# Twelve tiles of the second input layer as seven products, the convolution on VectorE, and the mixing between attention's layers

## The chip, the cores and the metric

One NeuronCore of one Trainium2 chip runs the whole program. The metric is the time of one execution on the device, in microseconds. The kernel before took 2616.39, 2611.67 and 2616.32 us in three runs; their median is 2616.32 us. All times below that come from a trace are of one profiled execution, which took 2621.87 us itself.

## The reference

Two transformer-like blocks stand behind each other, on 1024 tokens of 1024 features, in float32. The first has a state-space branch with a gated linear unit (GLU), an attention that lets each query look at the 256 best keys only (top-k of an index score), and a gated feed-forward layer (FFN). The second, which most of the change is about, has one wide input layer whose columns feed three branches:

```python
def second_block(x, ...):
    h = rmsnorm(x, norm_g)
    p = h @ w_in                                  # 1024 x 7688
    gate_pre, a_in, a_z, b_uv, b_z, q, k, v, c_z, f_pre = split_columns(p)
    gates = sigmoid(gate_pre + b_gate)            # 3 x 1024 columns
    # a: convolution of 31 taps over the tokens, a layer norm, a gate
    a = a_in[..., :512] * sigmoid(a_in[..., 512:])
    a = causal_depthwise_conv(a, conv_w, conv_b)
    y_a = (silu(layernorm(a)) * silu(a_z)) @ w_a
    # b: gMLP; tokens are mixed within chunks of 128
    u, v_b = split(b_uv)
    mixed = einsum("gts,bnsgc->bntgc", tril(w_s), chunks(rmsnorm(v_b))) + b_s
    y_b = (u * mixed * silu(b_z)) @ w_b
    # c: attention of 8 heads of 64 with a decay from the forget gate f_pre
    y_c = (fox_attention(rmsnorm(q), rmsnorm(k), v, cumsum(log_sigmoid(f_pre + b_f)))
           * silu(c_z)) @ w_c
    merged = g_a * y_a + g_b * y_b + g_c * y_c
    return x + merged @ w_out
```

## The kernel before, in words

**Arithmetic.** A float32 operand is split into a high and a low part of a shorter type (`split`: ScalarE copies the high part, VectorE or GpSimd subtracts it for the low part), and a product is three matmuls, high by high, high by low, low by high (`mm3`, L159 is its matmul, L167 is a transpose on TensorE). The helpers `act` (ScalarE, L130 to L132), `tt`, `stt` and `ts` (VectorE, L122, L125 and L119, or GpSimd where it is given as the engine) and `load` (a DMA on SP's queue, for stores too) record nearly every other operation.

**Layers.** A tile is 128 output features by 1024 tokens. `linear` makes one tile in 8 k-blocks x 2 halves of 512 tokens x 3 passes = 48 matmuls, into an accumulator `pl`, of which there are two. `wino` makes two tiles at once with 7 instead of 8 block products (a scheme of Strassen's kind), 7 x 4 x 3 = 84 matmuls into accumulators `pw`; each such job needs sums of weight blocks, split in high and low (`wino_weights`: tiles `vh`, `vl`, `s12`, `s34`), and its results are put together from accumulators and copies of them (`snap`). `linear_t` makes an output with tokens on the partitions, in groups of 256 columns of 192 matmuls. Four accumulators of 512 columns (`p`, from `p1()`) are shared by `linear_t`, by transposes and by the convolution's sums.

**What sets the order.** The program is written as one thread with side threads: a generator `self.aside` is advanced by `next` at fixed places, once per tile in `linear`, twice per job in `wino`, twice per group in `linear_t`. `together` mixes side threads at a given number of steps per call. A scheduler then orders the instructions of each engine by its own simulated times. Extra edges (`later`) keep a load or an operation behind a matmul, `self.pace` or `self.mark`.

**The first block's GLU** (`glu`, 16 tiles of 24 matmuls) runs with the side thread `attention1`: it loads and forms the heads' operands, then `topk`, then `attend`. The side thread is advanced by twelve steps during the GLU; what is left of it runs after. In `attend`, each step is a unit (head, block of 128 queries): `logits` (two or more matmuls into `pl`, softmax), `turn` (transposes of the weights), `weigh` (their product with the values).

**The second block** runs in this order: `conv_in` (the inputs of the convolution); `plain_gates` (8 tiles by `linear`: az, which is a_z, and c_z, which goes to the memory `fd`); `gates2` (24 tiles of gates by 12 seven-product jobs, with the convolution of tiles 0 and 1 as side thread); `fox` (attention's k, q and v by `linear_t`; the norms of k and q are generators in a list `pending`, which each group's eviction advances by `advance`); `gmlp` (branch b's v by `linear_t`, then z and u, 8 tiles by `linear`, with the mixing on TensorE between them); `branch` b. From `fox` to branch b the side thread is the convolution of tiles 2 and 3 (`conformer`), the gate of branch a (`conformer_gate`) and `keep_x2`, which transposes the block's input back to tokens. Then branch a, attention, branch c and the output layer follow.

**The convolution** (`conv`) runs one tap per instruction: 31 taps by two halves of 512 tokens are 62 operations on VectorE per tile, into an accumulator `p`. With `both` set (tiles 2 and 3), half the taps go to ScalarE (a scaled copy into `ct`) and GpSimd (an addition into `cy`).

Of the kernel before, what the change touches and what calls it, by code (L numbers as in the profile page):

```python
# [40 lines left out]
def blocks(x, c=128):  # L41
    return x.rearrange("p (b c) -> p b c", c=c)
# [26 lines left out]
class Core:  # L69
# [1532 lines left out]
    def keep_x2(self):  # L1602
# [17 lines left out]
    def fox(self, hh, hl):  # L1620
# [74 lines left out]
        for j, (c0, gain) in enumerate(((6656, self.v["k_norm_g_2"]), (6144, gq))):  # L1695
            for g in range(2):
# [30 lines left out]
                start(unit_norm(g, j, gain, x, ss))  # L1727
        for g in range(2):
# [11 lines left out]
            self.linear_t(self.wraw(w, 0, 8, 7168 + 256 * g, 256), 8, hh, hl, ev_v)  # L1740

    def plain_gates(self, hh, hl, norm):
# [4 lines left out]
        def ev(dst, scale):  # L1747
            def f(m, p):
                z = self.pg("gst", bufs=2)
                self.mark = self.act(z, p, AF.Tanh, scale=0.5)  # L1750
                self.stt(z, z, 1.0, p, OP.add, OP.mult)
                if scale != 1.0:
                    self.act(z, z, scale=scale)
                self.load(dst(m), z)
# [11 lines left out]
    def gates2(self, x4, first):  # L1766

# [3 lines left out]
        for pair in range(12):  # L1771
# [11 lines left out]
            jobs.append((lambda pair=pair: self.wino_weights(w, 256 * pair), ev))  # L1783
        self.wino(jobs, x4, first)
# [113 lines left out]
    def gmlp(self, hh, hl):  # L1898
# [5 lines left out]
        for g in range(2):  # L1904
            def ev_v(i, p):
                x = v[i][:, :, 256 * g:256 * g + 256]
# [6 lines left out]
        def mix(t):  # L1913
            if t == 0:
                self.tt(ss[:, 0], ss[:, 0], ss[:, 1], OP.add)
                r = self.rsqrt_cols(ss[:, 0], 512)
                for i in range(8):
                    x = v[i // 2][:, i % 2]
                    self.act(x, x, scale=r[:, i:i + 1])
            yield  # L1920
            mx = self.pg("bb", bufs=4)
            for s in range(2):
                q = blocks(self.p1())
                for i in range(4):
# [281 lines left out]
```

## Time and profile before

| | |
|---|---|
| runs | 2616.39, 2611.67, 2616.32 us, median 2616.32 |
| the profiled execution, its own time | 2621.87 us |
| its span in the trace | 2620.2 us |
| granted TensorE clock, mean | 0.984 |
| instructions | 35143 |
| seven products of the second block | 1720.2 to 1954.5 us |
| k, q and v of attention | 1954.5 to 2095.9 us |
| branch b's v | 2095.9 to 2155.4 us |
| z, u and the mixing | 2155.4 to 2266.4 us |
| branch b | 2266.4 to 2315 us |

PE is TensorE's matmul row, PEld its weight loads, DVE is VectorE, ACT ScalarE, POOL GpSimd, SP the queue that issues the DMAs. A group of instructions reads as line, engine, operation, output<-inputs by the program's names, shape, count, busy time, mean duration of one, and then the idle time of the engine just before it with what ended that. A matmul's duration in the trace overlaps that of the next, so the time of many is read from the stretch that they fill. In a table of waits, "PE pl L159 <- DVE small L1182: 8.8, 1, 8.8" says that TensorE's matmul of line 159 into the tile pl waited 8.8 us in one piece for VectorE's operation of line 1182 on the tile small. PEclk is the clock granted to TensorE as a share of full speed.

### The profile page before, as it was taken

Reading aid. Unit: us, or ns where it says so; the run is one execution under the profiler, and the core shown is the slowest. Engines: PE = TensorE matmul, PEld = TensorE weight load, DVE = VectorE, ACT = ScalarE, POOL = GpSimd, SP = SyncE. Lnnn points to the kernel's source line nnn. Section 1 sums busy time; section 2 is a strip of 40 time slices with the busy share of each in tenths; the row PEclk is TensorE's granted clock in tenths of the full one; section 3 lists DMA queues with packets and bytes.
Section 4 is the critical chain, followed back from the end, with each engine's and each line's share of the span. In section 5 each row is a group of like instructions: output and inputs, shape, how many; then the busy total and the mean of one; then the engine's idle time right before and its main releaser. Section 6 shows DMA issues by size and latency. Waiting matters only on the chain. (4 is left out here: it accounts for less than half of the span.)

```text
span 2620.2 us, 35143 instructions
## 1 busy us (share of the span) xinstructions
PE 2515.9 (96%) x12849; PEld 2119.9 (81%) x12849; DVE 1653.9 (63%) x2882; ACT 1129.7 (43%) x2144; POOL 847.9 (32%) x889
## 2 busy tenths in 40 slices
PE   6998999979999999999999999999999999999999
PEld 4877887768878788888888878888889997887887
DVE  6844889868894844444553367248768737548861
ACT  5323686828834433333322244234345433108830
POOL 2698441456500024444200120022318710005500
PEclk9999999989999999999999999999999999999999
DMA  7544453555294322222632244233362522586442
GB/s 256 158 152 139 143 167 112 192 168 132 73 332 154 124 90 89 70 91 81 223 135 85 87 131 149 85 105 121 113 206 77 166 77 73 183 235 156 135 159 83
DMA packets 272188, 360.37 MB, mean 138 GB/s; under 512 B 43948, under 2 KB 210552, under 8 KB 272016
## 3 DMA queue, kind: packets, MB, share of 16 engines
q1 hardware_dynamic: 270640, 356.89, 42.5%
q0 software_dynamic: 1152, 1.21, 0.3%
q8 instruction: 101, 1.65, 0.3%
q14 instruction: 71, 0.58, 0.1%
q10 hardware_dynamic: 224, 0.03, 0.0%
HBM read 262.65 MB, written 93.32 MB: 136 GB/s over the span
## 5 line engine op out<-in xcount | busy, mean ns | idle before, releaser
L130 ACT CAST wh<-wr 128x512 fp32r<-128x512 f32 (+1 forms) x308 | 170.7, 594 | 325.1 <-PE pl L159 125.9
L159 PE MATMUL pl<-uh,wh 128*128 128x512 f32 x672 | 266.6, 397 | 1.1 <-ACT uh L132 1.1
L159 PE MATMUL pl<-uh,wl 128*128 128x512 f32 x672 | 264.6, 394 | 0.6 <-DVE wl L122 0.6
L159 PE MATMUL pl<-ul,wh 128*128 128x512 f32 x672 | 263.9, 393 | 0.0
L122 POOL TENSOR_TENSOR s<-wq 128x512 f32<-128x512 f32 x60 | 84.8, 1415 | 480.1 <-DMA wq<-in_w_in_dram 268.6
L122 DVE TENSOR_TENSOR wl<-wr,wh 128x512 fp32r<-128x512 f32 (+1 forms) x260 | 179.1, 719 | 66.4 <-ACT wh L130 55.2
L122 DVE TENSOR_TENSOR snap<-pw,snap 128x512 f32<-128x512 f32 x90 | 61.9, 690 | 206.2 <-PE pw L159 116.9
L159 PE MATMUL pw<-xtl,vh 128*128 128x512 f32 x480 | 186.7, 389 | 0.0
L159 PE MATMUL pw<-xth,vl 128*128 128x512 f32 x480 | 185.3, 389 | 0.0
L159 PE MATMUL pw<-xth,vh 128*128 128x512 f32 x480 | 185.3, 389 | 0.0
L119 POOL TENSOR_SCALAR L<-L,small 128x128 f32<-128x128 f32 (+7 forms) x128 | 95.2, 747 | 259.8 <-DVE small L1186 253.1
L122 POOL TENSOR_TENSOR sqa<-sqa,sqn 128x512 f32<-128x512 f32 (+1 forms) x19 | 31.8, 1686 | 388.5 <-ACT sqn L132 206.8
L159 PEld LDWEIGHTS pl<-uh,wl 128*128 128x128 f32 x672 | 127.8, 190 | 27.7 <-DVE wl L122 1.1
L159 PE MATMUL p<-wth,uh 128*128 128x256 f32 x512 | 146.6, 287 | 3.1 <-DVE xsl L125 3.1
L159 PEld LDWEIGHTS pl<-uh,wh 128*128 128x128 f32 x672 | 127.6, 190 | 26.9 <-ACT uh L132 1.2
L159 PEld LDWEIGHTS pl<-ul,wh 128*128 128x128 f32 x672 | 127.9, 190 | 26.2 <-DVE ul L125 0.5
L159 PE MATMUL p<-wtl,uh 128*128 128x256 f32 x512 | 145.4, 284 | 0.0
L159 PE MATMUL p<-wth,ul 128*128 128x256 f32 x512 | 145.4, 284 | 0.0
L130 ACT COPY snap<-pw 128x512 f32<-128x512 f32 x90 | 52.6, 587 | 207.5 <-PE pw L159 196.6
L159 PE MATMUL pw<-uh,vh 128*128 128x512 f32 x360 | 140.0, 389 | 0.0
L159 PE MATMUL pw<-ul,vh 128*128 128x512 f32 x360 | 140.0, 389 | 0.0
L159 PE MATMUL pw<-uh,vl 128*128 128x512 f32 x360 | 136.6, 389 | 0.0
(448 smaller groups left out, 7264.0 us busy)
## 6 DMA issues: line engine op xcount, KB each, us to landing
wr<-in_w_in_dram SPq DMA_DIRECT2D x64, 512.0 KB, 4.8
wmod<-in_w_mod_dram SPq DMA_DIRECT2D x48, 512.0 KB, 6.3
wr<-in_w_out_dram SPq DMA_DIRECT2D x24, 512.0 KB, 6.2
wq<-in_w_in_dram SPq DMA_DIRECT2D x24, 512.0 KB, 5.2
gtd<-gst SPq DMA_DIRECT2D x24, 512.0 KB, 3.1
g_th<-gtd SPq DMA_DIRECT2D x24, 512.0 KB, 5.8
fd<-f_th SPq DMA_DIRECT2D x22, 512.0 KB, 3.4
f_th<-fd SPq DMA_DIRECT2D x22, 512.0 KB, 5.1
```

The costliest lines, as they stand in the source:

```text
L119: return (eng or self.nc.vector).tensor_scalar(out=out, in0=a, scalar1=s1, scalar2=s2, op0=op0, **kw)
L122: return (eng or self.nc.vector).tensor_tensor(out=out, in0=a, in1=b, op=op)
L130: return self.nc.scalar.copy(out, a)
L159: self.tick = self.nc.tensor.matmul(out, a, b, start=start, stop=stop, skip_group_check=True)
```

## The change

Five edits stand in it:

- Twelve tiles that `linear` made are now made by `gates2` in six more seven-product jobs (18 instead of 12): b_z (two jobs), u (two jobs) and c_z (two jobs). The product silu(b_z) * u is stored in a new memory `bf` and loaded back for the mixing; `plain_gates` keeps the four tiles of az.
- The convolution runs on VectorE alone, all 62 taps per tile. Three of its four tiles run beside the seven products (at 0.7 steps per call, was two tiles at 0.75), the last one in `conformer`.
- `gmlp` only makes branch b's v and returns the mixing as a generator, which `fox` puts into `pending`; it runs before attention's v, and the mixing between that layer's groups.
- `attention1` yields once more, between `topk` and `attend`.
- `keep_x2` loads one step ahead.

```diff
@@ keep_x2
-        for k in range(8):
+        ahead = []
+        def fetch(k):
             x = self.pg("h", bufs=8)
             self.load(x, self.hd2[k], self.pace)
             self.ts(x, x, fg[:, k:k + 1])
+            ahead.append(x)
+        fetch(0)
+        yield
+        for k in range(8):
+            x = ahead.pop(0)
+            if k < 7:
+                fetch(k + 1)
@@ fox
                 start(unit_norm(g, j, gain, x, ss))
+        start(self.gmlp(hh, hl, advance))
...
+        while pending:
+            advance()
@@ plain_gates
-        self.linear(w, [(4096 + 128 * t, 128) for t in range(4)], 8, hh, hl, ev(lambda m: self.az[m], 1.0))
-        self.linear(w, [(7680 + 128 * t, 128) for t in range(2)], 8, hh, hl, ev(lambda m: self.fd[m, 3, 0], 0.5))
+        self.linear(w, [(4096 + 128 * t, 128) for t in range(2)], 8, hh, hl, ev(0))
         first = self.wino_weights(w, 0, ref=self.tick)
-        self.linear(w, [(7680 + 128 * t, 128) for t in range(2, 4)], 8, hh, hl, ev(lambda m: self.fd[m + 2, 3, 0], 0.5))
+        self.linear(w, [(4096 + 128 * t, 128) for t in range(2, 4)], 8, hh, hl, ev(2))
@@ gates2
+        self.bf = self.dram([4, 128, T], "bf")
+        def silu(t, p, more):
+            if more is None:
+                more = p
+            else:
+                self.tt(more, p, more, OP.add)
+            self.mark = self.act(t, more, AF.Tanh, scale=0.5)
+            self.stt(t, t, 1.0, more, OP.add, OP.mult)
+        for pair in range(2):
...
+            def ev_z(m, s, p, more, g=g):
+                if g[m] is None:
+                    g[m] = self.pg("gst", bufs=2)
+                silu(g[m][:, 512 * s:512 * s + 512], p, more)
+            def ev_u(m, s, p, more, g=g, pair=pair):
+                t = g[m][:, 512 * s:512 * s + 512]
+                if more is None:
+                    self.tt(t, t, p, OP.mult)
+                else:
+                    self.tt(more, p, more, OP.add)
+                    self.tt(t, t, more, OP.mult, self.nc.gpsimd)
+                if (m, s) in ((0, 1), (1, 0)):
+                    self.load(self.bf[2 * pair + m], g[m])
+            jobs.append((lambda pair=pair: self.wino_weights(w, 5632 + 256 * pair), ev_z))
+            jobs.append((lambda pair=pair: self.wino_weights(w, 4608 + 256 * pair), ev_u))
+        for pair in range(2):
...
+            def ev_c(m, s, p, more, g=g, pair=pair):
...
+                silu(t, p, more)
+                self.act(t, t, scale=0.5)
+                if (m, s) in ((0, 1), (1, 0)):
+                    self.load(self.fd[2 * pair + m, 3, 0], g[m])
+            jobs.append((lambda pair=pair: self.wino_weights(w, 7680 + 256 * pair), ev_c))
@@ gmlp
-        def mix(t):
...
-        for t in range(4):
-            self.linear(w, [(5632 + 128 * t, 128)], 8, hh, hl, ev_z)
-            self.linear(w, [(4608 + 128 * t, 128)], 8, hh, hl, ev_u)
+        def mix():
+            self.tt(ss[:, 0], ss[:, 0], ss[:, 1], OP.add)
+            r = self.rsqrt_cols(ss[:, 0], 512)
...
+            for _ in range(4):
+                yield
+            for t in range(4):
+                f = self.pg("gz", bufs=2)
+                self.load(f, self.bf[t], self.pace)
+                mx = self.pg("bb", bufs=4)
+                for s in range(2):
...
+                self.tt(mx, mx, f, OP.mult)
+                self.bb.append(mx)
+                yield
+        return mix()
@@ conv
-        taps = range(30, -1, -2 if both else -1)
-        odd = list(range(29, -1, -2)) if both else []
...
-            for n, k in enumerate(taps):
+            for n, k in enumerate(range(30, -1, -1)):
...
-                        else:
-                            z = self.pg("ct", bufs=2)
-                            i = self.act(z[:, s:], at[:, :T - s], scale=wk)
-                            self.tt(y2[:, s:], y2[:, s:], z[:, s:], OP.add, gp)
...
-                if n % (4 if both else 8) == (3 if both else 7) and n < len(taps) - 1:
+                if n % 8 == 7:
                     yield
@@ conformer
-        yield from self.conv(2, True)
         x = self.cx
-        for t in range(2):
-            x[t] = self.pg("cx", bufs=4)
-            self.load(x[t], self.cyd[t], self.pace)
-        yield from self.conv(3, True)
...
+        for n, _ in enumerate(self.conv(3, True)):
+            if n == 3:
+                for t in range(3):
+                    x[t] = self.pg("cx", bufs=4)
+                    self.load(x[t], self.cyd[t], self.pace)
...
@@ run
             self.topk(self.sc)
+            yield
             yield from self.attend(self.heads1)
...
-        self.aside = self.together(((None for t in range(2) for _ in self.conv(t, False)), 0.75))
+        self.aside = self.together(((None for t in range(3) for _ in self.conv(t, False)), 0.7))
...
         self.fox(hh, hl)
-        self.gmlp(hh, hl)
```

**How the order moves, first place: TensorE, at the end of the GLU.** yl and yh are the GLU's inputs, wh and wl its weights, akh, akl and aqq the keys and queries of the first attention. Before, the first logits stand 96 matmuls ahead of the GLU's end:

```order
L159 MATMUL pl<-yl,wh 128x512
L159 MATMUL pl<-yh,wl 128x512
L159 MATMUL pl<-akh,aqq 128x256
L159 MATMUL pl<-akl,aqq 128x256
L159 MATMUL pl<-yh,wh 128x512
L159 MATMUL pl<-yl,wh 128x512
L159 MATMUL pl<-yh,wl 128x512
```

Now:

```order
L159 MATMUL pl<-yh,wh 128x512
L159 MATMUL pl<-yl,wh 128x512
L159 MATMUL pl<-yh,wl 128x512
L159 MATMUL pl<-akh,aqq 128x256
L159 MATMUL pl<-akl,aqq 128x256
L159 MATMUL pl<-akh,aqq 128x256
L159 MATMUL pl<-akl,aqq 128x256
L159 MATMUL pl<-akh,aqq 128x384
```

The first two logits matmuls have moved behind the last of the GLU, where those of the next unit follow them at once.

**Second place: GpSimd's queue (POOL), during attention's keys and queries.** wtl is the low part of a weight group, xraw the raw keys and queries, which the norm's factor is multiplied into there. Before:

```order
L122 TENSOR_TENSOR cy<-cy,ct 128x1017
L122 TENSOR_TENSOR cy<-cy,ct 128x1015
L122 TENSOR_TENSOR wtl<-wr,wth 128x1024
L122 TENSOR_TENSOR cy<-cy,ct 128x1013
L122 TENSOR_TENSOR cy<-cy,ct 128x1011
L122 TENSOR_TENSOR xraw<-xraw,small_16105 128x1024 x2
L122 TENSOR_TENSOR cy<-cy,ct 128x1009
L122 TENSOR_TENSOR cy<-cy,ct 128x1007
```

Now:

```order
L122 TENSOR_TENSOR xraw<-xraw,small_16711 128x1024 x2
L122 TENSOR_TENSOR wtl<-wr,wth 128x1024
L122 TENSOR_TENSOR xraw<-xraw,small_16711 128x1024 x2
L122 TENSOR_TENSOR sqa<-cx 128x1024
L122 TENSOR_TENSOR sqa<-sqa,cx 128x1024
L122 TENSOR_TENSOR wtl<-wr,wth 128x1024
L122 TENSOR_TENSOR xraw<-xraw,small_16711 128x1024 x2
```

The additions of the convolution are gone; weight splits, the norms' products and the two sums of the layer norm are left.

**Third place: VectorE, the chain of small operations behind the first group of keys** (the forget gate's and the first norm's; ca and p are the convolution's input and sum). Before:

```order
L119 TENSOR_SCALAR small_5047<-small_5047 128x64
L1637 RECIPROCAL small_5047<-small_5047 128x64
L1723 TENSOR_REDUCE small_5047<-sqk 128x8
L122 TENSOR_TENSOR small_5047<-small_5047 128x64
L119 TENSOR_SCALAR small_16105<-small_5047 128x32
L122 TENSOR_TENSOR small_5047<-small_5047 128x64
L119 TENSOR_SCALAR small_16105<-small_16105 128x32
```

Now:

```order
L125 SCALAR_TENSOR_TENSOR p_16585<-ca,small_5039,p_16585 128x502
L119 TENSOR_SCALAR small_5039<-small_5039 128x64
L119 TENSOR_SCALAR small_16711<-small_5039 128x32
L125 SCALAR_TENSOR_TENSOR p_16585<-ca,small_5039,p_16585 128x501
L1646 RECIPROCAL small_5039<-small_5039 128x64
L119 TENSOR_SCALAR small_16711<-small_16711 128x32
L125 SCALAR_TENSOR_TENSOR p_16585<-ca,small_5039,p_16585 128x500
L122 TENSOR_TENSOR small_5039<-small_5039 128x64
L119 TENSOR_SCALAR small_16711<-small_16711 128x32
L125 SCALAR_TENSOR_TENSOR p_16585<-ca,small_5039,p_16585 128x499
```

A tap of the convolution now stands between nearly every two operations of the chain.

## Rows read from the trace of the kernel before

**Rows 1.** The page: busy time, share of the span, and instructions of each engine.
```profile
PE 2515.9 (96%) x12849; PEld 2119.9 (81%) x12849; DVE 1653.9 (63%) x2882; ACT 1129.7 (43%) x2144; POOL 847.9 (32%) x889
```

**Rows 2.** TensorE's groups, 1633 to 1954 us: busy, mean ns | idle before.
```profile
L159 PE MATMUL pw<-xtl,vh 128*128 128x512 f32 x192 | 74.7, 389 | 0.0
...
L159 PE MATMUL pl<-uh,wh 128*128 128x512 f32 x128 | 49.8, 389 | 0.0
```

**Rows 3.** Windows by stage: us, busy of each engine (count), PEclk, DMA share, GB/s.
```profile
core 0: us, PE busy (x) PEld busy (x) DVE busy (x) ACT busy (x) POOL busy (x), PEclk, DMA share, GB/s
1633.13:1720.17 87.04, 87.04 (x385) 72.10 (x384) 25.68 (x27) 19.17 (x25) 8.51 (x6) 1.00 0.29 97
1720.17:1940.40 220.23, 220.23 (x973) 182.44 (x972) 163.00 (x215) 92.45 (x141) 60.48 (x44) 1.00 0.35 113
1954.50:2095.90 141.40, 131.60 (x1084) 130.80 (x1083) 105.91 (x165) 74.34 (x98) 103.00 (x45) 0.98 0.42 137
2095.90:2155.40 59.50, 59.50 (x500) 59.50 (x499) 20.34 (x26) 18.34 (x48) 6.49 (x3) 1.00 0.26 76
2155.40:2266.40 111.00, 105.87 (x515) 88.97 (x513) 70.54 (x94) 34.33 (x48) 4.77 (x2) 0.97 0.31 95
```

**Rows 4.** TensorE's waits in the GLU, 465 to 583 us: us, times, longest.
```profile
PE pl L159 <- DVE small L1182: 8.8, 1, 8.8
PE pl L159 <- POOL aqq L122: 3.3, 1, 3.3
```

**Rows 5.** TensorE's waits, 1954.5 to 2315 us.
```profile
PE p L167 <- POOL xraw L122: 5.3, 1, 5.3
PE pl L167 <- ACT diag L130: 4.1, 1, 4.1
PE p L159 <- DVE xsl L125: 3.1, 1, 3.1
PE pl L167 <- DVE small L125: 1.4, 1, 1.4
```

**Rows 6.** Windows behind two waits, and of the first attention.
```profile
558.40:563.80 5.40, 5.40 (x13) 4.25 (x14) 1.10 (x2) 0.42 (x2) 4.22 (x5) 0.51 0.74 272
582.90:715.60 132.70, 119.60 (x811) 104.56 (x809) 111.88 (x318) 113.45 (x269) 84.03 (x140) 0.97 0.45 114
2075.10:2079.30 4.20, 4.16 (x20) 4.16 (x21) 2.10 (x5) 3.01 (x4) 4.15 (x2) 0.51 0.63 182
```

**Rows 7.** VectorE's groups beside the seven products, and the FFN's activation (f_th).
```profile
L125 DVE SCALAR_TENSOR_TENSOR p<-ca,small,p 128x512 f32<-128x512 f32 x60 | 45.1, 752 | 1.2
L122 DVE TENSOR_TENSOR vl<-s,vh 128x1024 fp32r<-128x1024 f32 x22 | 32.2, 1462 | 3.2 <-ACT vh L130 3.0
L122 DVE TENSOR_TENSOR snap<-pw,snap 128x512 f32<-128x512 f32 x35 | 24.1, 690 | 46.2 <-PE pw L159 27.0 <-ACT snap L130 18.9
L122 DVE TENSOR_TENSOR vl<-wq,vh 128x512 fp32r<-128x512 f32 x33 | 21.8, 685 | 1.3 <-ACT vh L130 1.3
...
L125 DVE SCALAR_TENSOR_TENSOR f_th<-f_th,snap x27: 677/695/1782, 960.7 to 1283.7; 128x512 f32<-128x512 f32 x27
```

**Rows 8.** A window of one job's length, VectorE alone.
```profile
1758.20:1777.30 19.10, 17.38 (x25) 1.00 0.37 111
```

**Rows 9.** TensorE's timeline, the matmul behind the first logits.
```profile
558.34 0.80 PE L159 MATMUL pl<-yh,wh 128*128 128x512 f32 x1 [8.77 <-DVE small L1182]
```

**Rows 10.** Tiles cy and wtl: count, ns least/median/most, first and last start.
```profile
L122 POOL TENSOR_TENSOR cy<-cy,ct x28: 2337/2393/4356, 1965.2 to 2097.4; 128x1021 f32<-128x1021 f32 x2, 128x1019 f32<-128x1019 f32 x2, 128x1017 f32<-128x1017 f32 x2, 128x1015 f32<-128x1015 f32 x2
...
L122 DVE TENSOR_TENSOR wtl<-wr,wth x7: 1220/2048/3461, 1944.3 to 2109.7; 128x1024 fp32r<-128x1024 f32 x7
```

**Rows 11.** VectorE's timeline: start, us; how a norm's chain opens, at two places.
```profile
2034.14 0.60 DVE L119 TENSOR_SCALAR small<-small 128x32 f32<-128x32 f32 x3
...
2063.46 5.04 DVE L119 TENSOR_SCALAR small<-small 128x32 f32<-128x32 f32 x3
```

**Rows 12.** VectorE's groups, 1954 to 2100 us: the forget gate's running sum.
```profile
L1652 DVE TENSOR_TENSOR_SCAN kin<-kiw,small 8x1024 f32<-8x1024 f32 x1 | 3.3, 3295 | 0.0
```

More of the change, by code (lines that the diff above doesn't have):

```diff
@@ L1905, in ev_v @@
             def ev_v(i, p):
+                advance()
                 x = v[i][:, :, 256 * g:256 * g + 256]
@@ L1911, in gmlp @@
         self.bb = []
-        def mix(t):
[L1914 to L1924, printed above, removed]
-                    self.mm(q[:, i], v[2 * s + i // 2][:, i % 2, t * 128:(t + 1) * 128], wst[:, t * 128:(t + 1) * 128])
-                self.stt(blocks(mx[:, 512 * s:512 * s + 512]), q, self.v["gmlp_norm_g_2"][:, t:t + 1],
-                         wst[:, None, 512 + 128 * t:640 + 128 * t].to_broadcast([128, 4, 128]), OP.mult, OP.add)
-            self.bb.append(mx)
-            yield
@@ L1930, in gmlp @@
-        steps = (None for t in range(4) for _ in mix(t))
-        self.hold = []
-        def ev_z(m, p):
-            th = self.pg("gz", bufs=2)
-            self.act(th, p, AF.Tanh, scale=0.5)
-            self.stt(th, th, 1.0, p, OP.add, OP.mult)
-            self.hold.append(th)
-            next(steps)
-        def ev_u(m, p):
-            th = self.hold.pop(0)
-            self.tt(th, th, p, OP.mult)
-            next(steps)
-            t = len(self.bb) - 1
-            self.tt(self.bb[t], self.bb[t], th, OP.mult)
-            self.show(f"bb{t}", self.bb[t])
@@ L1947, in gmlp @@
-        for t in range(4):
-            self.linear(w, [(5632 + 128 * t, 128)], 8, hh, hl, ev_z)
-            self.linear(w, [(4608 + 128 * t, 128)], 8, hh, hl, ev_u)
+        def mix():
+            self.tt(ss[:, 0], ss[:, 0], ss[:, 1], OP.add)
+            r = self.rsqrt_cols(ss[:, 0], 512)
+            for i in range(8):
+                x = v[i // 2][:, i % 2]
+                self.act(x, x, scale=r[:, i:i + 1])
+            for _ in range(4):
[5 more added lines that the diff above has]
+                for s in range(2):
+                    q = blocks(self.p1())
+                    for i in range(4):
+                        self.mm(q[:, i], v[2 * s + i // 2][:, i % 2, t * 128:(t + 1) * 128], wst[:, t * 128:(t + 1) * 128])
+                    self.stt(blocks(mx[:, 512 * s:512 * s + 512]), q, self.v["gmlp_norm_g_2"][:, t:t + 1],
+                             wst[:, None, 512 + 128 * t:640 + 128 * t].to_broadcast([128, 4, 128]), OP.mult, OP.add)
+                self.tt(mx, mx, f, OP.mult)
+                self.bb.append(mx)
+                self.show(f"bb{t}", mx)
+                yield
@@ L1978, in conv_in, with conv @@
             part(2, s)
-    def conv(self, t, both):
-        gp, cw = self.nc.gpsimd, self.cw
+    def conv(self, t, keep):
+        cw = self.cw
         at = self.pg("ca", bufs=4)
@@ L1986, in conv @@
         y = self.pg("cx", bufs=4)
-        taps = range(30, -1, -2 if both else -1)
-        odd = list(range(29, -1, -2)) if both else []
-        if both:
-            y2 = self.pg("cy", bufs=2)
-            self.later(gp.memset(y2[:, 0:1], 0.0), self.pace)
         for h in range(2):
@@ L2002, in conv @@
                 self.later(i, self.pace)
[L2003 to L2020 removed]
+                if n % 8 == 7:
+                    yield
+            self.act(y[:, c0:c0 + 512], acc)
             if h == 1:
                 self.show(f"conv{t}", y)
[L2023 removed]
+                if keep:
                     self.cx[t] = y
@@ L2031, in conformer @@
         gp = self.nc.gpsimd
[L2032 removed]
         x = self.cx
[L2034 to L2041 removed]
+        for n, _ in enumerate(self.conv(3, True)):
[3 more added lines that the diff above has]
+                    self.load(x[t], self.cyd[t], self.pace)
+                total = self.pg("sqa", bufs=4)
+                for y in (x[0], total):
+                    self.later(self.tt(total, y, x[1] if y is x[0] else x[2], OP.add, gp), self.pace)
+            yield
         self.tt(total, total, x[3], OP.add)
@@ L2126, in attention1 @@
             self.topk(self.sc)
+            yield
             yield from self.attend(self.heads1)
```

34 lines of the change are left out of this document (10 added, 24 removed).

## The prediction

> **What bounds the kernel now.** I read the page first: TensorE is busy for 96% of the span and VectorE for 63% [rows 1]. A busy matmul row is not yet a full engine, since rows overlap, so I take the price of a matmul from its pitch. The groups of the stretch that the change touches have no idle time before them, neither in the plain tiles (pl) nor in the tiles by seven products (pw) [rows 2]. In the windows by stage, 384 plain matmuls fill 87.04 us and 972 of the seven products 220.23 us [rows 3]: 0.2267 us each, in both. There, only fewer matmuls save time. Elsewhere TensorE stands still, and I looked for where: its own waits name 8.8 and 3.3 us in the GLU of the first block [rows 4] and 5.3, 4.1, 3.1 and 1.4 us between the end of the seven products and branch b [rows 5]. After a wait the granted clock is low for a while: 5.40 us at 0.51 hold 13 matmuls [rows 6], which at the pitch above take 2.9. So a wait costs its length and some half-speed matmuls (1.2 instead of 2.4 GHz).
>
> **The change, part by part.**
>
> *Seven products for twelve tiles.* A plain tile is 48 matmuls (8 k, 2 halves, 3 passes), so 576 go; six jobs of 84 come, 504. 72 x 0.2267 = **16.3 us less**, if the new jobs run without idle time as the old ones do.
>
> What has to hide beside them is VectorE's work. A job with a gate's activation has, from the rows of VectorE [rows 7]: two wide splits (1.46) and three narrow ones (0.685), 5.0 us; two additions of a snap (0.69), 1.4; four products of the activation (0.695, the row f_th of the FFN), 2.8; and its share of the convolution. Three parts of 62 taps over 36 calls at 0.7 steps of 8 taps are about 11 taps a job, at 0.752, 8.4 us. Together 17.6 us in the 19.04 us that 84 matmuls take: 92%. One old stretch of that length already carries 17.38 us [rows 8], and TensorE never waited there. So I cost it at nothing; the cover that is left is 1.4 us a job. The other queues have room: POOL is busy 60 of 220 us and ACT 92 [rows 3], and get four products of 512 columns (1.4 us each, 60.48 / 44) and some 24 activations (0.7 us, 92.45 / 141). SP's queue gets four stores and four loads of 512 KB, at DMA shares of 0.26 to 0.42 there.
>
> The Trainium skill, in "Perfetto Trace Analysis", section "Optimizing Scalar/DVE Operations", advises the opposite of the convolution's move: where VectorE is saturated, hand work to ScalarE or GpSimd. By it the six full jobs would lose time; the rival on VectorE below works out how much.
>
> *The added yield.* The twelfth step of the first attention now ends with top-k; the first logits, two matmuls, stand behind the GLU's last 142 matmuls instead of ahead of its last 96, as the first pair of pieces of the order shows. Today those two wait 3.3 us for POOL's aqq, and the next matmul 8.8 us, because the logits hold one of two accumulators until VectorE is through with top-k; it starts at 558.34 [rows 4, 9]. The 13 matmuls that follow at half clock cost 5.40 - 13 x 0.2267 = 2.5 us [rows 6]. All three go: 14.6 us. VectorE is through with top-k by 558, and the GLU, which now ends where attention's stretch begins at 582.9, would end at about 568.3, so nothing is late there. What comes back is the first unit of attention, which is not yet done when the others start. It costs at least nothing and at most a mean unit, 132.7 / 63 = 2.1 us (8 heads by 8 blocks, less this one) [rows 6]; it is the smallest of its head, so I take half, 1.1. **13.5 us less**, 12.5 to 14.6.
>
> *The convolution leaves POOL and ACT.* In the stretch of keys and queries, 28 additions of about 2.4 us on POOL go [rows 10], and as many scalings on ACT. VectorE's taps there stay: 62 for one tile instead of 2 x 32 for two. The rows show what the additions did. The three small operations that open VectorE's chain for a norm take 0.60 us at 2034 and 5.04 us at 2063 [rows 11]; POOL has no addition at the first place and a run of them at the second. A split of 1.22 us took up to 3.46 beside them [rows 10]. That chain is what the wait of 5.3 us hung on. The waits in this stretch sum to 13.9 us [rows 5], and the half clock behind them costs 2.1 us (half of 4.20 at 0.51) [rows 6] and 3.3 us (3% of 111) in the stage of z and u [rows 3]: 19.3 us in all. How much goes?
>
> The 5.3 with its clock should go. The 4.1 is a transpose placed too close behind a chain of small operations; in the new order 57 matmuls of 256 columns stand between, 6.8 us at 59.50 / 500 = 0.119 a piece [rows 3], and VectorE's chain is 12 operations of about 0.2 and three others, 5 us with ACT's copy; it should go, barely. The 1.4 goes, since its transposes now stand 63 matmuls later. The 3.1 is a matmul without an accumulator, since two convolution sums and two transposes hold all four. That stays, and between the two pieces it waits for VectorE now has four taps, a split, a reduction and a scan (3.3 [rows 12]), some 9 us; I put it at 5, and 2 for the clock behind. So 12 of 19 go. Bounds: nothing goes (0), or all (19). **12 us less.**
>
> A risk stands in the third pair of pieces: the taps are now mixed into the first norm's chain, ten of them at 0.75 us in 13 us. POOL's product follows, at most an addition's 2.4 [rows 10], so its transposes are ready some 15 to 17 us after the first group ends, where TensorE reaches them after 144 matmuls, 17.1 us.
>
> *The mixing* keeps its 64 matmuls and moves between the groups of attention's v. Its inputs pass through VectorE (two sums of 0.75, a product and a split of 1.22, and v's own split of 0.69, by the rows of like width [rows 7, 10]: 4.6 us) in the 5.7 us of 48 matmuls of 256 columns: no wait, no gain. *The loads of keep_x2* start one earlier, but its eight steps come closer together, at the start of branch b: three passes of VectorE each, about 0.7 a 512 columns, beside the two of a branch tile, 4.5 us in the 5.4 of its 24 matmuls. Nothing, up to 5 us of loss.
>
> Sum: 16.3 + 13.5 + 12 = 41.8 us. The profiled execution took 2621.87 us, so 2580.1; it lies 5.55 us above the median of the runs (2616.32), which gives **2574.5 us** as the median after.
>
> **The rivals.**
> 1. *The stretch of keys and queries gives nothing*: taps in the norm chains, and the closer steps of keep_x2, cost what POOL's additions did. For it: VectorE is busy 106 of 141 us there already [rows 3]. Against: the waits are tied to operations beside the additions. 2616.3 - 16.3 - 13.5 = 2586.5.
> 2. *VectorE becomes the bound of the six full jobs.* If both wide splits met POOL at 3.46 instead of 1.46, a job needs 21.6 us against 19.04: 2.6 x 6 = 15 us back, 2590. It decides from 1.4 us more than I count. Against: 17.38 us passed without a wait [rows 8]. This is what the skill's advice would come to.
> 3. *Slower: the same in all 18 jobs.* The taps fall in all of them; if the splits late by that much stop TensorE in each, 2.6 x 18 = 47 us come back: 2621.5. It needs VectorE over 19.04 us in every job, and today the mean is 163.00 / 220.23 of it, 14.1 [rows 3].
> 4. *The yield moves the wait, and the attention ends no sooner*, because it is bound from its start by VectorE and ScalarE (112 and 113 of 132.7 us [rows 6]). Against: TensorE is busy 120 of the same 132.7, and VectorE is idle when the GLU ends. 2588.
>
> **How the numbers follow.** Forecast 0.60 (its own range 2566 to 2584: 19 or 3 of the 19.3 us go, and the yield's bounds), rival 1 0.20, rival 2 0.10, rival 4 0.06, rival 3 0.04. The range of 8 in 10 takes in the forecast and the first two rivals and reaches past both: down by the 4 us or so that the three runs differ among themselves (2566 - 4), up by the same and most of keep_x2's 5 (2590 + 8): 2562 to 2598. A measurement of this kernel can tell about 0.2%, 5 us, from no change. All but rival 3 and the far end of rival 2 are faster by more: 0.93 faster, 0.03 same, 0.04 slower.
>
> **What would show it.** Seven products: 1476 pw matmuls in one block of about 335 us at 0.2267, no waits of pw. Yield: no wait of TensorE in the GLU, its end near 568 us, first block's attention still about 133 us. Stretch: no operation of a norm's chain above 0.3 us, one wait for xsl of 3 to 6 us. I am wrong if pw matmuls wait for vl or snap, or if the waits between the seven products and the third branch sum to more than 15 us.

## The result, and the profile after

The changed kernel takes 2577.81 us (median of four runs, 2574.54 to 2580.82), the kernel before 2616.36 in the same comparison: 0.986 of the time, 95% interval 0.9848 to 0.9872, or 38.6 us less. The forecast was 2574.5, with a range of 2562 to 2598. The profiled execution took 2580.82 us (before: 2621.87), so the two traces differ by 41.1 us of span, against a sum of 41.8.

The total hides that two of its three terms were far off, in opposite directions. The page of the changed kernel, for [rows 1]:

```profile
PE 2495.0 (97%) x12777; PEld 2106.2 (82%) x12777; DVE 1697.6 (66%) x2968; ACT 1120.5 (43%) x2152; POOL 821.5 (32%) x889
```

72 matmuls are gone. VectorE carries 43.7 us more work, GpSimd 26.4 less. To see where the time went I cut both traces at the same places of the program and compare stretches. The kernel before, the GLU, and all from the last of the seven products to the end of branch b (the first attention stands in [rows 6]):

```profile
core 0: us, PE busy (x) PEld busy (x) DVE busy (x) ACT busy (x) POOL busy (x), PEclk, DMA share, GB/s
465.24:582.89 117.65, 103.00 (x438) 83.17 (x437) 86.44 (x138) 60.95 (x133) 65.26 (x34) 0.94 0.53 173
1940.49:2314.98 374.49, 358.69 (x2402) 331.18 (x2401) 224.25 (x320) 139.65 (x214) 116.93 (x52) 0.98 0.43 139
```

The changed kernel: the GLU, the first attention, the plain tiles, the seven products, and the stretch behind them to the end of branch b:

```profile
466.86:580.72 113.86, 102.22 (x436) 82.70 (x434) 86.65 (x134) 60.28 (x129) 64.13 (x31) 0.96 0.54 178
580.72:713.18 132.46, 119.56 (x814) 105.14 (x813) 111.69 (x322) 114.83 (x272) 84.97 (x143) 0.97 0.43 115
1628.25:1671.77 43.52, 43.52 (x194) 36.04 (x192) 15.97 (x15) 7.90 (x10) 9.29 (x7) 1.00 0.29 97
1671.77:2006.33 334.56, 334.56 (x1478) 277.03 (x1476) 255.70 (x331) 135.35 (x209) 106.75 (x74) 1.00 0.33 109
2006.33:2272.71 266.38, 264.59 (x2018) 254.47 (x2016) 184.49 (x302) 97.29 (x169) 43.94 (x21) 1.00 0.57 187
```

From the stretch before I take off the 384 plain matmuls of z and u, 87.05 us at 0.2267, since they now stand as seven products:

| step | forecast | by the two traces |
|---|---|---|
| twelve tiles as seven products | 16.3 | 16.3 (43.52 + 334.56 against 87.04 + 220.32 + 87.05) |
| GLU and first attention (the yield) | 13.5 | 4.0 (113.86 + 132.46 against 117.65 + 132.70 [rows 6]) |
| end of the seven products to the end of branch b | 12 | 21.1 (266.38 against 374.49 - 87.05) |
| everything else | 0 | -0.3 |

The last row hides a spread: the way from the first attention into the FFN, which no edit touches, is 2.5 us shorter in the second trace (235.55 against 238.02), and other parts are longer. So a difference of 2 us in one stretch of two traces shows nothing by itself.

*Seven products.* 1476 matmuls fill 334.56 us, 0.2267 each as before, and no row of pw has a wait. VectorE's heaviest new jobs (windows of one job's length, as [rows 8]):

```profile
1918.50:1937.50 19.00, 18.14 (x22) 1.00 0.20 56
1937.50:1956.50 19.00, 16.93 (x24) 1.00 0.32 110
```

The job that I had put at 17.6 us takes 17 to 18, and TensorE does not notice.

*The GLU.* Of its waits, for [rows 4], one has taken the place of the two:

```profile
PE pl L159 <- POOL wl L122: 10.6, 3, 8.6
```

*Keys, queries, v, mixing, branch b*, for [rows 5]: of the waits there nothing over 1.5 us is left, and that one is new and small. The clock column says 1.00, where it was 0.98.

```profile
PE pl L159 <- DVE wtl L122: 1.5, 1, 1.5
```

### The profile page after: what moved, and what is told of

It is laid out like the page before. It is cut to its first block, busy times and chain, and to the rows that moved or that the text cites. A ratio compares the mean times of both kernels' runs of the same rounds, so it can differ in the third digit from the quotient of the medians.

```text
span 2579.1 us, 35104 instructions
## 1 busy us (share of the span) xinstructions
PE 2495.0 (97%) x12777; PEld 2106.2 (82%) x12777; DVE 1697.6 (66%) x2968; ACT 1120.5 (43%) x2152; POOL 821.5 (32%) x889
## 3 DMA queue, kind: packets, MB, share of 16 engines
q0 software_dynamic: 1152, 1.21, 0.3%
## 4 chain that ended last, share of the span: by engine, by line
PE 78%; DVE 10%; POOL 4%; ACT 3%; DMA 2%; issue 2%; SPq 0%; POOLq 0%; DVEq 0%; ACTq 0%
PE pw L159 26%; PE pl L159 24%; PE p L159 24%; PE p L167 3%; DVE tk_j L119 2%; POOL s_F L122 1%; POOL s_ct L122 1%; POOL s_E L122 1%; ACT L L132 1%; DVE s_d L122 1%; DVE h L125 1%; DMA yd<-s_X 0%; PE pl L167 0%; DMA aq<-qd 0%; DVE wl L122 0%
## 5 line engine op out<-in xcount | busy, mean ns | idle before, releaser
L159 PE MATMUL pw<-xtl,vh 128*128 128x512 f32 x576 | 224.1, 389 | 0.0
L159 PE MATMUL pw<-xth,vh 128*128 128x512 f32 x576 | 222.8, 389 | 0.0
L159 PE MATMUL pw<-xth,vl 128*128 128x512 f32 x576 | 222.3, 389 | 0.0
L122 DVE TENSOR_TENSOR wl<-wr,wh 128x512 fp32r<-128x512 f32 x236 | 160.0, 708 | 59.5 <-ACT wh L130 50.4
L159 PE MATMUL pl<-uh,wh 128*128 128x512 f32 x480 | 190.9, 399 | 1.1 <-ACT uh L132 1.1
L159 PE MATMUL pl<-uh,wl 128*128 128x512 f32 x480 | 189.5, 395 | 0.0
L159 PE MATMUL pl<-ul,wh 128*128 128x512 f32 x480 | 188.4, 393 | 0.0
L125 DVE SCALAR_TENSOR_TENSOR p<-ca,small,p 128x512 f32<-128x512 f32 (+9 forms) x240 | 177.9, 743 | 4.1
L159 PEld LDWEIGHTS pw<-xth,vl 128*128 128x128 f32 x576 | 108.1, 188 | 22.4
L159 PEld LDWEIGHTS pw<-xth,vh 128*128 128x128 f32 x576 | 108.1, 188 | 22.4
```

Of the source, the lines that this page charges most:

```text
L122: return (eng or self.nc.vector).tensor_tensor(out=out, in0=a, in1=b, op=op)
L125: return self.nc.vector.scalar_tensor_tensor(out=out, in0=a, scalar=s, in1=b, op0=op0, op1=op1)
L159: self.tick = self.nc.tensor.matmul(out, a, b, start=start, stop=stop, skip_group_check=True)
```

## The experiments

Twelve kernels, each timed beside the kernel before, whose median lay between 2614.3 and 2616.7 us; a variant is compared with the changed kernel's 2577.8, and 2 us between two of them mean nothing (the changed kernel's own four runs spread over 6). Where the question is in one stretch, I compare the length of the stretch in the traces.

### The yield: which wait came next?

GpSimd's queue in the changed kernel, around the new wait (start, duration, in brackets the idle time before):

```profile
546.07 2.39 POOL L122 TENSOR_TENSOR g_th<-g_tg,g_th 128x1024 f32<-128x1024 f32 x1 [7.00 <-DVE small L426]
548.54 2.60 POOL L122 TENSOR_TENSOR aqq<-aq,aqq 64x1024 fp32r<-64x1024 f32 x1
551.23 3.13 POOL L119 TENSOR_SCALAR g_tg<-g_tg 128x1024 f32<-128x1024 f32 x1
554.33 2.52 POOL L122 TENSOR_TENSOR wl<-wr,wh 128x512 fp32r<-128x512 f32 x1
```

and TensorE's matmul that waited for the last of them:

```profile
556.91 0.79 PE L159 MATMUL pl<-yh,wl 128*128 128x512 f32 x1 [8.57 <-POOL wl L122]
```

wl is the low part of the next GLU weights. It stands behind g_tg, aqq and the gate product g_th, and g_th had stood still for 7.0 us because its input passes through VectorE, whose queue is full of top-k:

```profile
543.64 1.15 DVE L125 SCALAR_TENSOR_TENSOR tk_eq<-sc,small,tk_eq 128x896 bf16<-128x896 f32 x1
544.71 1.22 DVE L125 SCALAR_TENSOR_TENSOR g_th<-g_th,g_val 128x1024 f32<-128x1024 f32 x1
```

The same four rows stand in the trace before, 2.1 us earlier. The last of them there:

```profile
552.20 2.52 POOL L122 TENSOR_TENSOR wl<-wr,wh 128x512 fp32r<-128x512 f32 x1
```

So wl ended at 554.72, and TensorE, held by the logits, went on at 558.34 [rows 9]. By this the logits' wait covered another that was only 3.6 us shorter. That is the theory; three kernels test it.

**e1_no_yield**, the changed kernel without the yield:

```diff
             self.topk(self.sc)
-            yield
```

> The changed kernel without the added yield. Theory (GpSimd's chain): the changed kernel already waits 8.6 us in the GLU for the weights' low part, which GpSimd makes behind the gate products that wait for VectorE, so the yield only took the 3.3 us wait for aqq and what the logits held beyond that chain. Without it the GLU is about 4 us longer, with 3.3 and 8.8 us of waits as before: 2582. Rival (the sum of the prediction): 13.5 us come back, 2591.

2579.58 us, 0.9862 of the kernel before (0.9845 to 0.988). The two old waits are back in its trace, and the time is 1.8 us from the changed kernel's, within noise. Nothing like 13.5 us comes back.

```profile
PE pl L159 <- DVE small L1182: 8.5, 1, 8.5
PE pl L159 <- POOL aqq L122: 3.3, 1, 3.3
```

**e2_before_yield**, the kernel before with the yield alone:

```diff
             self.topk(self.sc)
+            yield
```

> The kernel before with the added yield alone. Theory (GpSimd's chain): about 4 us less, 2612, with one wait of some 8 to 9 us for GpSimd's wl in the GLU. Rival (the sum of the prediction): 13.5 us less, 2603, with no wait in the GLU.

2613.53 us against 2614.57, 0.9992 (0.9983 to 1.0). Its waits in the GLU:

```profile
PE pl L159 <- POOL wl L122: 10.4, 3, 8.5
```

The same wait as in the changed kernel. In the runs the yield is worth 1 to 2 us, which is not clear of noise. In the traces it is: the GLU and the first attention together take 250.4 to 250.7 us in the four kernels without the yield (before, e1, e9, e11) and 246.3 to 248.6 in the eight that have it and the GLU as it was, some 2 to 4 us less.

**e3_glu_vector**, the changed kernel with one operation on VectorE for two on GpSimd:

```diff
-            self.ts(tg, tg, 1.0, None, OP.add, eng=self.nc.gpsimd)
-            self.tt(th, tg, th, OP.mult, self.nc.gpsimd)
+            self.stt(th, tg, 1.0, th, OP.add, OP.mult)
```

> The changed kernel with the GLU's (1 + tg) * th as one operation on VectorE instead of two on GpSimd, so that GpSimd's wl stands behind nothing that waits for VectorE. Theory (GpSimd's chain): the wait of 8.6 us and its half clock go, 2567 to 2570. Rival (the weights' load, ScalarE's high part or top-k itself hold TensorE): the wait stays within 2 us of 8.6, 2576 to 2580.

2571.22 us, 0.9828 (0.9812 to 0.9845): 6.6 us faster than the changed kernel, 1.2 us short of what the theory wanted. The wait for wl is gone, and the next one shows, half as long:

```profile
PE pl L159 <- DVE small L426: 4.3, 1, 4.3
PE p L167 <- POOL L L119: 3.2, 2, 2.3
```

Line 426 copies small vectors of the second block out of an accumulator, also behind top-k.

**e12_glu_params** takes that away too:

```diff
-        self.params2()
...
         for _ in att:
             pass
+        self.params2()
```

> The changed kernel with the GLU's gate product on VectorE (as e3_glu_vector) and the second block's vectors fetched after the first attention, so that their transposes do not hold an accumulator until VectorE copies it behind top-k. Theory (the wait of 4.3 us that was left in e3_glu_vector hung on that copy): no wait over 2 us in the GLU, 4 to 7 us less than e3_glu_vector: 2564 to 2568. Rival (something else of top-k holds it): 2569 to 2573.

2570.93 us, 0.9822 (0.9809 to 0.9836): no different from e3. The expected 4 to 7 us did not come, though the wait went as expected and the GLU is shorter (103.35 us, e3 108.21). In the trace other stretches are longer: the first attention is 1.1 us longer, with a longer wait for the softmax's scaling on GpSimd, and the way from there to the FFN 2.7 us. (That way also ranges from 228.2 to 232.4 us in the other traces, so the 2.7 may be chance. Where the gain went stays open.)

```profile
PE p L167 <- POOL L L119: 4.8, 2, 3.9
```

### The stretch of keys and queries: is it GpSimd's additions?

In the changed kernel most of VectorE's small operations and weight splits are short. The kernel before, VectorE's group of 128x32 from 1954 to 2160 us:

```profile
L125 DVE SCALAR_TENSOR_TENSOR small<-small 128x32 f32<-128x32 f32 x24 | 8.7, 361 | 0.6
```

The changed kernel, the same group from 2006 to 2160 us:

```profile
L125 DVE SCALAR_TENSOR_TENSOR small<-small 128x32 f32<-128x32 f32 x24 | 4.5, 187 | 0.4
```

The split wtl has a median of 1221 ns, where [rows 10] had 2048. Not all are short: GpSimd still has its own splits and products there, and beside its two products that start at 2054.55 an operation of the first norm's chain takes 1.31 us, where most of its kind take 0.22.

```profile
2057.10 1.31 DVE L125 SCALAR_TENSOR_TENSOR small<-small,small 128x64 f32<-128x64 f32 x1
```

But the changed kernel also has fewer taps and accumulators in use there, and the mixing lies elsewhere. **e10_idle_adds** changes GpSimd alone:

```diff
+        if keep:
+            y2, z = self.pg("cy"), self.pg("ct")
+            for x in (y2, z):
+                self.later(self.nc.gpsimd.memset(x, 0.0), self.pace)
...
                 self.later(i, self.pace)
+                if keep and n % 4 == 3:
+                    self.later(self.tt(y2, y2, z, OP.add, self.nc.gpsimd), self.pace)
```

> The changed kernel with 14 additions of 1024 columns on GpSimd that nobody reads, at the places where the last convolution part has its taps; VectorE's work and the accumulators are untouched. Theory (it is GpSimd's additions as such): VectorE's operations of 128x32 go from a mean of 0.19 us to 0.3 or more, the stretch gets 4 to 10 us longer: 2582 to 2588. Rival (accumulators held by the halved taps, or the sums that wait for GpSimd at the end of a part): nothing changes, 2576 to 2580.

2588.82 us, 11 more than the changed kernel and just above the expected range; the stretch takes 276.98 us instead of 266.38. Additions that nobody reads cost it two waits:

```profile
PE pl L167 <- DVE small L125: 4.0, 1, 4.0
PE p L159 <- ACT xraw L130: 3.7, 1, 3.7
```

How they do it stands in the timelines of this kernel. GpSimd:

```profile
2038.60 2.40 POOL L122 TENSOR_TENSOR wtl<-wr,wth 128x1024 fp32r<-128x1024 f32 x1
2040.96 5.86 POOL L122 TENSOR_TENSOR cy<-cy,ct 128x1024 f32<-128x1024 f32 x2
```

VectorE, at the same time:

```profile
2038.61 3.47 DVE L122 TENSOR_TENSOR wtl<-wr,wth 128x1024 fp32r<-128x1024 f32 x1
2042.00 0.73 DVE L125 SCALAR_TENSOR_TENSOR p<-ca,small,p 128x503 f32<-128x503 f32 x1
2042.65 1.77 DVE L122 TENSOR_TENSOR small<-small 128x64 f32<-128x64 f32 x1
2044.34 0.67 DVE L1732 TENSOR_REDUCE small<-sqk 128x8 f32<-128x512 f32 x1
2044.93 0.73 DVE L125 SCALAR_TENSOR_TENSOR p<-ca,small,p 128x502 f32<-128x502 f32 x1
2045.58 1.29 DVE L119 TENSOR_SCALAR small<-small 128x64 f32<-128x64 f32 x1
```

The split starts with GpSimd's own split, ends 1.1 us after it, and so has its usual 1.2 us only once GpSimd is through. The product of 128x64, 0.21 us in the changed kernel, ends at 2044.42, which is when the first addition ends if its 2.4 us start with the end of VectorE's split (the two additions together take 5.86 us, 1.1 more than twice 2.4). The last row ends with the second addition. Between them the taps take their 0.73 us, as without additions: one of their two large operands is the accumulator p. So it isn't a slower VectorE; some operations stand still until GpSimd's ends, and others don't.

Against the changed kernel the three held operations are 2.3, 1.6 and some 1.1 us longer, and GpSimd's product behind that chain starts later by about as much. In e10, whose stretch starts at 2003.37, and in the changed kernel, where it starts at 2006.33:

```profile
2056.26 3.76 POOL L122 TENSOR_TENSOR xraw<-xraw,small 128x1024 f32<-128x1024 f32 x2 [9.44 <-DVE small L125]
2054.55 3.77 POOL L122 TENSOR_TENSOR xraw<-xraw,small 128x1024 f32<-128x1024 f32 x2 [12.95 <-DVE small L125]
```

That is 52.9 us into the stretch against 48.2, 4.7 later. GpSimd stood idle before it in both, so its queue was not what made it late.

The Trainium skill says this in "SBUF — State Buffer", section "Who interferes with whom": a VectorE instruction with two inputs in SBUF (the memory in which all tiles but the accumulators lie) contends with a GpSimd instruction that reads SBUF, one with at most one such input, outside the modes that use both ports, doesn't, and the port that the two engines share is locked, not shared out. The trace agrees: 3.47 us for the split, 0.73 for the tap. Whether the TENSOR_SCALAR of the last row, held with a single input in SBUF, ran in such a mode, no row shows.

The expected mean of 0.3 us or more came for the products of 128x32 (0.331, 0.186 in the changed kernel), not for the group above (188 ns), which met no addition.

**e4_one_part_split** gives the last part's odd taps back to ScalarE and GpSimd, with `conv` as it was before (`both` for the last part) and the rest as changed:

```diff
-            for n, k in enumerate(range(30, -1, -1)):
+            for n, k in enumerate(taps):
...
+                            i = self.act(z[:, s:], at[:, :T - s], scale=wk)
+                            self.tt(y2[:, s:], y2[:, s:], z[:, s:], OP.add, gp)
```

> The changed kernel with every second tap of the last convolution part on ScalarE and GpSimd, as before: 14 additions on GpSimd come back beside the keys and queries, and 31 of VectorE's 62 taps go. Theory (the additions slow VectorE's operations): the small operations of 128x32 go from a mean of 0.19 us to 0.3 or more, the weights' split from 1.2 to 2 us or more, and TensorE waits 3 to 8 us in the stretch again: 2581 to 2587. Rival (the stretch got faster because VectorE and the accumulators have less to hold, or because the mixing moved): no wait over 2 us comes back, 2575 to 2579.

2587.74 us, 10 more than the changed kernel, with 30 taps fewer on VectorE (16 of 31 stay in each half); the stretch takes 274.30 us. The group of 128x32 is back at its old length:

```profile
L125 DVE SCALAR_TENSOR_TENSOR small<-small 128x32 f32<-128x32 f32 x24 | 8.8, 365 | 0.6
```

The split of 1024 columns takes a mean of 2.2 us, 1.5 in the changed kernel. The wait for an accumulator that the forecast wanted to keep is back, and one for the small operations:

```profile
PE p L159 <- DVE xsl L125: 3.4, 1, 3.4
PE pl L167 <- DVE small L125: 2.0, 1, 2.0
```

**e11_conv_only** makes the convolution's edit alone on the kernel before:

```diff
-        self.aside = self.together(((None for t in range(2) for _ in self.conv(t, False)), 0.75))
+        self.aside = self.together(((None for t in range(3) for _ in self.conv(t, False)), 1.0))
```

with `conv` and `conformer` of the changed kernel.

> The kernel before with the convolution's edit alone (VectorE alone, three parts beside the twelve jobs at one step a call, the last in the stretch; z and u stay plain tiles). Theory (the additions slow the stretch): the waits for xraw (5.3) and xsl (3.1) go with their half clock, no wait of pw: 8 to 14 us less, 2600 to 2607. Rival (the convolution's edit pays only together with the others): within 4 us of before, 2610 to 2618.

2602.66 us against 2616.73, 0.9946 (0.9934 to 0.9959): 14 us, without any of the other edits. In the trace the stretch takes 356.88 us instead of 374.49, 17.6 less. Of [rows 5] only one wait is left, at the same place as the one for xsl (a matmul without an accumulator), under another name:

```profile
PE p L159 <- ACT cx L130: 3.2, 1, 3.2
```

### Do the parts add up?

**e9_tiles_only** is the kernel before with the seven products for the twelve tiles and nothing else; the mixing then stands behind attention's layers with no tiles between its pieces. Of its edit, the last hunk:

```diff
-        self.gmlp(hh, hl)
+        for _ in self.gmlp(hh, hl, lambda: None):
+            pass
```

> The kernel before with the twelve tiles by seven products alone (their silu and the product with u with them); convolution, yield and keep_x2 as before, and the mixing behind attention's layers with nothing left between its pieces. Theory (the 87 us of plain z and u tiles were the cover of the mixing and of the convolution's tail): the 16.3 us are more than given back, 2610 to 2625. Rival (the prediction's terms add up): 16.3 us less, 2598 to 2602.

2619.69 us against 2616.73, ratio 1.0007 (0.9997 to 1.0018): 72 matmuls fewer, and no gain. The 16.3 us are there in the window of the seven products. From its end to the end of branch a 9.2 us are lost again (340.13 against 374.49 + 43.52 - 87.05), and 5.4 in all that follows (267.1 against 261.7). (The whole traces differ by 5.7 us the other way: this profiled execution lies 3.5 us below its median, the one before 5.5 above. The runs decide.) The first entries of the waits behind the seven products:

```profile
PE p L159 <- ACT gv L132: 13.1, 1, 13.1
PE pl L159 <- DVE attl L125: 4.0, 3, 2.0
PE p L167 <- POOL xraw L122: 3.2, 1, 3.2
```

The longest is the mixing's, for the normed v (gv), and before there was none for it: the z and u tiles were the cover under which the norm of v ran.

**e6_mix_after** is the changed kernel with the same place for the mixing:

```diff
-        start(self.gmlp(hh, hl, advance))
...
         self.fox(hh, hl)
+        for _ in self.gmlp(hh, hl, lambda: None):
+            pass
```

> The changed kernel with branch b's v and the mixing behind all of attention's layers instead of between them. Theory (the move hides the mixing's inputs): the mixing waits for the norm of v, for VectorE's sums and for the loads of bf: 5 to 12 us more, 2583 to 2590. Rival (the move is worth nothing, as the prediction costed it): within 3 us, 2575 to 2581.

2591.46 us, 13.6 more than the changed kernel, just above the theory's range. The stretch is 280.55 us, with the same two waits first, that for gv shorter than in e9; none is for the loads of bf:

```profile
PE pl L159 <- DVE attl L125: 4.8, 3, 3.0
PE p L159 <- ACT gv L132: 4.2, 1, 4.2
```

**e5_conv_back** is the changed kernel with the old convolution, so seven products, mixing between the layers, and 28 additions (`conv`, `conformer` and the rate as before):

```diff
-        self.aside = self.together(((None for t in range(3) for _ in self.conv(t, False)), 0.7))
+        self.aside = self.together(((None for t in range(2) for _ in self.conv(t, False)), 0.75))
```

> The changed kernel with the convolution as before (two parts beside the seven products, two in the stretch with half their taps on ScalarE and GpSimd, 28 additions). Theory (the additions slow the stretch): 14 to 20 us come back, 2592 to 2598, with waits for xraw and xsl of 3 us or more. Rival (the mixing's move between attention's layers carried the gain): at most 6 us come back, 2578 to 2584.

2607.67 us, 30 more, above both expectations. Beside the waits of the additions there is a new one, for the column sums of the convolution's layer norm: without the z and u tiles the longer work beside the stretch does not end in time and runs into branch b.

```profile
PE p L159 <- POOL sqa L122: 6.2, 1, 6.2
PE p L167 <- POOL xraw L122: 4.1, 1, 4.1
PE pl L159 <- DVE g_th L125: 3.5, 2, 3.2
```

**e7_keep_old** undoes only the early loads of `keep_x2` (the first hunk of the diff above).

> The changed kernel with keep_x2 as before. Theory (the prediction's: nothing): 2575 to 2580. Rival (its loads were late at the start of branch b, where the mixing ends earlier now): 3 us or more slower, 2581 to 2586.

2583.89 us (2580.85 to 2589.13), 6 more. By the ratios it is 4 (0.9874, 0.9859 to 0.9889, against 0.986, 0.9848 to 0.9872), and the intervals overlap. The stretch is 272.23 us, 5.8 longer, as the rival has it; the first transpose waits for the scaled input, which stands behind the mixing's operations on VectorE:

```profile
PE p L167 <- DVE h L119: 4.2, 1, 4.2
```

### Is VectorE the next bound of the seven products?

**e8_four_parts** puts the last part of the convolution beside them as well:

```diff
-        self.aside = self.together(((None for t in range(3) for _ in self.conv(t, False)), 0.7))
+        self.aside = self.together(((None for t in range(4) for _ in self.conv(t, False)), 0.95))
```

with `conformer` loading all four parts.

> The changed kernel with all four parts of the convolution beside the seven products (0.95 steps a call instead of 0.7). By the sum's working VectorE then needs 20.4 us in each of the six full jobs against 19.04 of TensorE. Theory (VectorE bounds job by job): waits of pw for vl or snap of 6 us or more in the last six jobs, 2582 to 2590. Rival (buffers carry the excess over to lighter jobs): no waits, 2575 to 2579.

2606.03 us, 28 more: neither number. In the seven products the rival was right: VectorE is busy for 18.7 us or more in each of the last four windows of 19, and the 1476 matmuls have no wait. One of the four:

```profile
1926.00:1945.00 19.00, 18.86 (x26) 1.00 0.35 124
```

The loss lies behind them, where VectorE lost 62 taps: 292.09 us for the stretch, 25.7 more, with long waits that the changed kernel doesn't have.

```profile
PE p L167 <- POOL xraw L122: 7.8, 1, 7.8
PE p L159 <- POOL sqa L122: 7.0, 1, 7.0
PE p L167 <- DVE h L119: 3.4, 1, 3.4
```

The layer norm's steps, which the taps used to hold back, now come at the first calls of the side thread, and TensorE's column sums stand in its queue ahead of keys and queries before GpSimd has their operand. That the order of steps is the cause is argued from these rows; a variant with empty steps in the taps' place was not run.

## Why the prediction was right, and where it was not

**Seven products: right in size and in VectorE's share.** 16.3 us forecast, 16.3 in the trace; no wait for VectorE. The rival that VectorE bounds the six full jobs was given 0.10; in e8 VectorE is 99% busy there, and TensorE still did not wait. What the step left out is that the tiles which became cheaper were somebody else's cover: alone they are worth nothing (e9).

**The yield: wrong, 4.0 instead of 13.5.** The step that failed is "All three go: 14.6 us", with "so nothing is late there" behind it. I checked when top-k and the GLU would end, but not who else was waiting while TensorE stood still. GpSimd's wl ended at 554.72 in the very trace that I read, 3.6 us ahead of the end of the wait, and about that difference is what came. Rival 4 had the right consequence (the wait moves) and the wrong place: it looked behind the GLU, in attention, and the new wait stands inside it.

**The stretch: right mechanism, too small, 21.1 instead of 12.** GpSimd's additions as the cause are shown by e10 (put in alone they cost 11 us) and by e11 (the convolution's edit alone brings 14, and 17.6 of this stretch in the trace). 21.1 lies past the upper of the two bounds, 0 and 19. By the windows TensorE's idle time fell by 14.0 us (15.8 to 1.8), and its busy time, apart from the plain tiles, by 7.1 (271.6 to 264.6), for which I had 5.4 of half clock. The step that failed is "The 3.1 ... stays ... I put it at 5, and 2 for the clock behind": nothing of these 7 us is left. Why not stays open. In e11, also with one part of the convolution in the stretch, 3.2 us of that wait are left. e1, e6 and e7 don't have it, so none of the yield, the mixing's place and the loads of keep_x2 took it away alone; between the twelve tiles and the rate of the taps no run decides. One sign failed as well, "no operation of a norm's chain above 0.3 us": one takes 1.31.

Two edits that I costed at nothing hold losses off: without the move of the mixing ("no wait, no gain") 13.6 us come back (e6), without the loads of keep_x2 ("Nothing, up to 5 us of loss") 4 to 6 (e7). They are no part of the surplus, since before there was no wait for gv or h. I compared the mixing with the kernel before, where the z and u tiles still covered it. For keep_x2 I added up VectorE's time and didn't ask where the scaled input stands in its queue.

**The Trainium skill's advice.** I weighed the half of "Perfetto Trace Analysis", section "Optimizing Scalar/DVE Operations", that hands work from VectorE to other engines. The next sentence there reminds the reader that GpSimd and VectorE share a read port, so that moving work between those two might not help. It is this sentence that the trace agrees with (3.47 against 1.21 us for the split).

So the sum was 0.7 us off by the traces because an error of 9.5 us one way met one of 9.1 us the other. That is luck. (The other 2.6 of the 3.3 us between forecast and median come from the step from trace to median: the profiled execution lay 5.5 us above its median before, 3.0 after.) The range would have held with either error alone: 2587 without the stretch's surplus, 2568 without the yield's shortfall.

## What to carry to other kernels

Before you book a wait as gone, list what else ends while the engine stands still: the gain is about the distance to the next late releaser, which the trace before already shows. When tiles get cheaper, ask what ran under them, and price the edits that come along against the kernel that will be left, not against the one you profile. Work given to GpSimd is not free because GpSimd is idle: look at how long VectorE's two-operand operations take beside it.

The fastest version here is the changed kernel with the GLU's gate product as one operation on VectorE (e3_glu_vector): 2571.22 us, 0.9828 of the kernel before, 6.6 us better than the change; e12, at 2570.93, is no different.

## What the runs showed of the hardware that I had not expected

In e10's trace some VectorE operations that meet an addition on GpSimd are held to its end, even if they are 0.2 us long: a product of 128x64 took 1.77 us instead of 0.21 beside an addition of 2.4 us, while a tap of 503 columns, 0.73 us long, ran through. So it isn't their size that decides in these rows. The two with both inputs in SBUF, the split and the product, were held; the tap, with one of its two large inputs in an accumulator, was not. The number of inputs doesn't settle it alone: with one input, the TENSOR_SCALAR of 128x64 was held (1.29 us) and the reduction of 512 columns was not (0.67). A tap on VectorE, with its sum in an accumulator, was never held in these rows, while additions on GpSimd hold back the small operations that TensorE waits for (4.0 us in e10, 2.0 in e4).
